# Attention's background work in another order, queries in a scaled tile of their own, and bias loads at fixed places

## The chip, the cores and the metric

The kernel runs on one core of one Trainium2 chip. Engines: TensorE (PE), VectorE (DVE), ScalarE (ACT), GpSimd (POOL) and SyncE (SP, which here only issues DMAs). The metric is device time in microseconds, the median of several runs.

## What is computed

A two-layer decoder trunk on 512 tokens of 1024 features, float32 in and out. Layer 0 is a short gated convolution and a squared-ReLU MLP. Its output is normalised once and projected into one set of keys and values for the attention of layer 1. That attention has 16 heads of 64 in 4 groups, and three branches that share the queries: compressed blocks, selected blocks and a window. A relative-position bias is added to every logit. A second MLP and a final norm follow. The part that matters here, cut to its core:

```python
def compress_blocks(t, pe, w1, w2):      # t: (S, G, 64) raw keys or raw values
    chunks = t.reshape(S // 16, 16, G, 64)
    blocks = concat([chunks[:-1], chunks[1:]]) + pe        # 31 blocks of 32 tokens
    return silu(flat(blocks) @ w1) @ w2                    # the "block MLP": 2048 -> 256 -> 64

kv = (h @ w_kv).reshape(S, 6, G, 64)     # raw k, raw v, selected k, v, window k, v
k_cmp, v_cmp = compress_blocks(kv[:, 0], ...), compress_blocks(kv[:, 1], ...)
q, gates = split(h @ w_qg); q = q * 64 ** -0.5
for branch in (compressed, selected, window):
    p = softmax(q @ k.T + bias)          # causal
    o += gate[branch] * (p @ v)
x = x + o @ w_o
```

With 8 blocks of 64 tokens and the 16 best to be taken, every block is selected, so the selected branch is full causal attention.

## The kernel before, in words

**Numbers.** Every large product is done in float16 halves: a float32 operand is split into a high part (ScalarE, a scaled copy) and a low part (VectorE, `x*scale - high`), and PE does three matmuls, high by high, high by low, low by high (`mm3`, L355 to L358).

**Weights.** A list of pieces of 512 KB is written out in the order of use (L105 to L132). SP loads them, three buffers ahead (`load_piece`). `convert_piece` splits one into `whi` (L202) and `wlo` (L203). `next_piece` hands out the next one; `ahead_fine` (L714) converts the piece behind it in halves, as a generator that the caller steps between matmuls.

**The lead-in of attention** (L926) runs in a row: keys of the two full branches, queries of group 0, values of both, gates.

**Items and background.** After that the work of a group is cut into items. A `Full` item is one block of 128 queries, one branch and as many heads as fit in 512 columns of logits; a `Cmp` item is one block of 128 queries and two groups against the 31 compressed blocks. There are 96 items: 22 of group 0, 22 of group 1, 26 of group 2 with four `Cmp` among them, 26 of group 3 with four. Each item goes through stages `st0` to `st4`, and the loop at L1164 interleaves them: in turn i it runs `st0` of item i, `st1` of item i − 2, `st2` of i − 3, `st3` of i − 4, `st4` of i − 6.

- `st0`: scores on PE into bank b (two buffers; L998, L999), then on VectorE the bias and the row minimum in one instruction per head (L1006: out `at_s`, in `b` and `T`), then the exponent on ScalarE (L1008: out `at_p`).
- `st1`: transposes on PE into bank c (L1014) and the high part on ScalarE (L1017). `st2`: the low part on VectorE (L1020).
- `st3`: the product with the values on PE into bank d (L1033 to L1035), scaling on VectorE (L951, `o_t`), sums on POOL (L953, L956). `st4`: transposes (L967) and the split into `big` for the output projection.

Between items a generator, `background()` (L1147), is stepped for as long as a credit lasts. A step of it is some matmuls with a price (0.65 for one chunk of a projection, 0.42 for one of the block MLP), and each turn adds to the credit (L1174). Its order: raw keys, queries 1, block MLP of the keys (`phi(0)`), raw values, queries 2, block MLP of the values (`phi(1)`), queries 3, then, when groups 0 and 1 are finished (`o1`), the first half of the output projection. An item that needs something not yet done runs the background until it is.

**Queries** (L775). The projection lands in banks a. Per pair of heads VectorE scales it into a tile of 512 columns from the rotating pool `at_s` (L688, three buffers, the same name as the logits'). Per head, ScalarE writes the high half into `Q` (L785), and POOL the low half (L786), both from that tile. **Raw keys and values** (L793) go through `at_s` too (L804), are split into `kr_hl` and moved by DMA into `big`, which the block MLP reads. **The block MLP** (L818) accumulates its two halves in two banks a. **Bias tiles** `T` hold four heads' biases for one group; `load_T` issues their load on ScalarE's queue ahead of item 11, 35 and 60.

The framework that records the kernel orders each engine's instructions itself; `tc.issue_after(x)` keeps an instruction behind another one.

## Time and profile before

| | us |
|---|---|
| runs shown: 1113.25, 1115.03, 1116.88, median | 1115.03 |
| profiled execution, its own time | 1114.4 |
| its span, first to last instruction | 1112.5 |
| PE busy | 1091.4 |
| VectorE busy | 869.6 |
| ScalarE busy | 572.4 |
| POOL busy | 58.6 |

Attention's items run from about 549 to 760 us of the span. Lines are those of the kernel before. In a row of a view, `out<-in` are the program's tiles, x is a count, and what stands behind `<-` in brackets ended the engine's idle time. A matmul's end is modelled and matmuls are pipelined, so short waits of PE do not show as idle time.

### The profile page before, as it was taken

To read this page: it belongs to the slowest core of one execution; us is meant where nothing else is said; L and a number is where in the kernel's file an instruction comes from. 1 tells how busy PE (TensorE), PEld (TensorE's weight loads), DVE (VectorE), ACT (ScalarE), POOL (GpSimd) and SP (SyncE) were. 2 spreads that over 40 slices of the span, in tenths; PEclk is the share of its full clock that TensorE was granted. 3 is DMA by queue.
4 is the path that set the end of the run, shared out by engine and by line. 5 is a ranking of instruction groups with operands and counts; after the bars stand their busy time and mean duration, and the time that the engine had idled before them with its cause. 6 is when DMAs were issued, how large, how long until landed. Compare 5 with 4: busy or idle time off the path is not lost.

```text
span 1112.5 us, 20040 instructions
## 1 busy us (share of the span) xinstructions
PE 1091.4 (98%) x7960; PEld 694.1 (62%) x7960; DVE 869.6 (78%) x1627; ACT 572.4 (51%) x923; POOL 58.6 (5%) x75
## 2 busy tenths in 40 slices
PE   9999999999999999999999999899999999999996
PEld 4444444446884448875767676675444788445895
DVE  5755457987998677969588889997998698865776
ACT  4622235545343444447578787875754433352353
POOL 1000000000000000000102021212000000000020
PEclk9999999999999999999999999999999999999998
DMA  6433335543334333313334241112653333330221
GB/s 215 131 98 99 110 96 151 154 125 105 111 118 119 103 98 106 103 30 111 118 98 135 68 128 59 39 40 71 182 158 101 101 120 112 108 94 1 96 77 76
DMA packets 149708, 115.74 MB, mean 104 GB/s; under 512 B 8700, under 2 KB 146640, under 8 KB 149616
## 3 DMA queue, kind: packets, MB, share of 16 engines
q1 hardware_dynamic: 146624, 108.88, 32.2%
q10 hardware_dynamic: 2608, 4.97, 1.4%
q8 instruction: 62, 1.02, 0.4%
q0 software_dynamic: 384, 0.63, 0.2%
q14 instruction: 30, 0.25, 0.1%
HBM read 110.22 MB, written 2.14 MB: 101 GB/s over the span
## 4 chain that ended last, share of the span: by engine, by line
PE 86%; DVE 7%; ACT 3%; issue 2%; POOL 1%; DMA 0%; DVEq 0%; ACTq 0%; SPq 0%
PE a L582 8%; PE c L582 8%; PE a L357 6%; PE a L356 6%; PE a L358 6%; PE b L582 6%; PE c L356 6%; PE c L358 6%; PE c L357 6%; PE b L358 6%; PE b L357 5%; PE b L356 5%; PE d L582 4%; PE e L582 2%; PE c L1014 2%
## 5 line engine op out<-in xcount | busy, mean ns | idle before, releaser
L202 ACT ACTIVATE whi<-wst 128x1024 f16<-128x1024 f32 (+3 forms) x172 | 144.3, 854 | 188.1 <-PE b L357 66.4
L203 DVE SCALAR_TENSOR_TENSOR wlo<-wst,whi 128x1024 f16<-128x1024 f32 (+3 forms) x172 | 169.5, 996 | 44.8 <-ACT whi L202 44.5
L582 PEld LDWEIGHTS <-whi 128*128 128x128 f16 x1792 | 175.3, 98 | 20.6
L358 PEld LDWEIGHTS <-wlo 128*128 128x128 f16 x1024 | 100.3, 98 | 111.5 <-issue 0.5
L357 PEld LDWEIGHTS <-whi 128*128 128x128 f16 x1024 | 100.2, 98 | 108.7 <-issue 2.8
L356 PEld LDWEIGHTS <-whi 128*128 128x128 f16 x1024 | 100.4, 98 | 107.9 <-issue 0.9
L189 ACT ACTIVATE whi<-wst 128x1792 f16<-128x1792 f32 x64 | 108.5, 1700 | 109.2 <-DVE wst L187 43.6
L190 DVE SCALAR_TENSOR_TENSOR wlo<-wst,whi 128x1792 f16<-128x1792 f32 x64 | 129.0, 2018 | 14.4 <-ACT whi L189 14.4
L187 DVE TENSOR_TENSOR wst<-wst 128x256 f32<-128x256 f32 x256 | 95.7, 421 | 19.5 <-DMA wst<-mlp_w_dram 18.2
L533 DVE TENSOR_TENSOR rl<-ml_z,rh 128x1792 f16<-128x1792 f32 x32 | 64.8, 2024 | 44.7 <-ACT rh L532 44.7
L582 PEld LDWEIGHTS <-wlo 128*128 128x128 f16 x896 | 87.7, 98 | 10.8 <-issue 0.2
L532 ACT ACTIVATE rh<-ml_z 128x1792 f16<-128x1792 f32 x32 | 54.3, 1696 | 57.2 <-DVE ml_z L531 57.2
L1008 ACT ACTIVATE at_p<-at_s,at_m 128x384 f32<-128x384 f32 (+3 forms) x128 | 70.8, 554 | 21.4 <-DVE at_m L1006 20.5
L357 PE MATMUL b<-xsl,whi 128*128 128x512 f16 x208 | 78.8, 379 | 0.0
L358 PE MATMUL b<-xsh,wlo 128*128 128x512 f16 x208 | 78.8, 379 | 0.0
L356 PE MATMUL b<-xsh,whi 128*128 128x512 f16 x208 | 78.7, 379 | 0.0
L356 PE MATMUL c<-xsh,whi 128*128 128x512 f16 x192 | 72.8, 379 | 0.0
L357 PE MATMUL c<-xsl,whi 128*128 128x512 f16 x192 | 72.8, 379 | 0.0
L358 PE MATMUL c<-xsh,wlo 128*128 128x512 f16 x192 | 72.8, 379 | 0.0
L582 PE MATMUL c<-rl,whi 128*128 128x256 f16 x256 | 69.8, 273 | 0.0
L582 PE MATMUL c<-rh,whi 128*128 128x256 f16 x256 | 69.8, 273 | 0.0
L582 PE MATMUL c<-rh,wlo 128*128 128x256 f16 x256 | 69.8, 273 | 0.0
(318 smaller groups left out, 2549.0 us busy)
## 6 DMA issues: line engine op xcount, KB each, us to landing
wst<-mlp_w_dram SPq DMA_DIRECT2D x256, 256.0 KB, 3.3
wst<-a_w_in_dram SPq DMA_DIRECT2D x18, 512.0 KB, 3.6
wst<-w_kv_dram SPq DMA_DIRECT2D x12, 512.0 KB, 3.6
T<-ext_d ACTq DMA_DIRECT2D x4, 1056.0 KB, 6.1
wst<-a_w_out_dram SPq DMA_DIRECT2D x8, 512.0 KB, 3.4
wst<-b_w_qg_dram SPq DMA_DIRECT2D x8, 512.0 KB, 3.6
wst<-b_w_o_dram SPq DMA_DIRECT2D x8, 512.0 KB, 3.3
wst<-a_w_in_dram SPq DMA_DIRECT2D x7, 384.0 KB, 5.0
```

The source lines that it names most:

```text
L187: DVE.tensor_tensor(b[:, :, o], b[:, :, x], b[:, :, y], op=e)
L189: ACT.activation(hi, b[:, :, 1:], AF.Copy, scale=sc)
L190: DVE.scalar_tensor_tensor(lo, b[:, :, 1:], sc, hi, op0=OP.mult, op1=OP.subtract)
L202: ACT.activation(hi[:, s:e], w, AF.Copy, scale=sc)
L203: DVE.scalar_tensor_tensor(lo[:, s:e], w, sc, hi[:, s:e], op0=OP.mult, op1=OP.subtract)
L356: PE.matmul(ps, w[0], xs[0], start=start, stop=False)
L357: PE.matmul(ps, w[0], xs[1], start=False, stop=False)
L358: return PE.matmul(ps, w[1], xs[0], start=False, stop=stop)
L532: ACT.activation(rh[0][:, p], z[:, 1:8], AF.Copy)
L533: DVE.tensor_tensor(rh[1][:, p], z[:, 1:8], rh[0][:, p], op=OP.subtract)
L582: mm = PE.matmul(acc7[i], wl if n == 1 else wh, xl if n == 2 else xh, stop=c == 7 and n == 2, start=c == 0 and n == 0 and not other, skip_ ...
L1008: ACT.activation(self.p[:, w], lg[:, w], AF.Exp, bias=mn[:, j:j + 1], scale=-1.0, accum_out=l[:, br * 4 + h:br * 4 + h + 1])
```

## The change

- Weight pieces of the keys' block MLP and of the raw values are listed alternately, and `in_turn(phi(0), raw(1))` steps the two generators alternately. Since two generators are then open, the running conversion is held in one place (`fine`) and drained before the next piece is handed out.
- The block MLP's two halves share one bank e in place of two banks a.
- Queries are scaled into `q_t`, a tile of two times 512 columns with one buffer; raw keys and values and the second block MLP use the same name. The four splits into high and low halves are queued (`later`), and the loop runs one per item. An item waits for the heads that it uses. The low half of groups 1 and 2 is on VectorE, of groups 0 and 3 on POOL.
- The bias loads are issued behind the exponent of items 8, 29 and 58.
- The first four `Cmp` items stand behind items 4, 7, 10 and 13 of group 2 in place of 9 to 12. The credit per item is 1.14, 0.9 and 0.68 in place of 1.03, 0.78, 0.8 and 0.65.

```diff
-    block(phi_k_w1, 0, SW, 0, 16)
+    for k in (0, 8):
+        block(phi_k_w1, 0, SW, k, 4)
+        cols(w_kv, 256, 256, SW, k // 2, 4)
+        block(phi_k_w1, 0, SW, k + 4, 4)
     cols(phi_k_w2, 0, 64, SW, 0, 2)
-    block(w_kv, 256)
...
         pos["use"] += 1
+        drain(fine[0])
         while i not in ready:
...
         def ahead_fine():
-            while pos["cv"] < min(pos["use"] + AHEAD, len(pieces)):
-                yield from convert_piece(512)
+            drain(fine[0])
+            def convert():
+                while pos["cv"] < min(pos["use"] + AHEAD, len(pieces)):
+                    yield from convert_piece(512)
+            fine[0] = convert()
+            return fine[0]
...
             q = ap.tile([128, 4, S], F16, name="Q", bufs=3)
+            t = ap.tile([128, 2, S], F32, name="q_t", bufs=1)
+            Qs[g] = q
+            def head(h):
+                m, s = h // 2, h % 2
+                r, o = slice(64 * s, 64 * s + 64), slice(64 - 64 * s, 128 - 64 * s)
+                ACT.activation(q[r, h], t[r, m], AF.Copy)
+                (POOL if g in (0, 3) else DVE).tensor_tensor(q[o, h], t[r, m], q[r, h], op=OP.subtract)
+                done.add(f"q{g}.{h}")
             for m in range(2):
-                t = scaled(po[m], rbq)
-                for s in range(2):
-                    h, r = 2 * m + s, slice(64 * s, 64 * s + 64)
-                    o = slice(64 - 64 * s, 128 - 64 * s)
-                    ACT.activation(q[r, h], t[r], AF.Copy)
-                    POOL.tensor_tensor(q[o, h], t[r], q[r, h], op=OP.subtract)
-                yield
-            Qs[g] = q
+                DVE.tensor_tensor(t[:, m], po[m], rbq, op=OP.mult)
+            for h in range(4):
+                if lead_in[0]:
+                    head(h)
+                else:
+                    later.append(lambda h=h: head(h))
+            yield
...
-            ph = [bank("a"), bank("a")]
+            pb = bank("e")
+            ph = [pb[:, 0:155], pb[:, 155:310]]
...
-        items += mixed(full(2, (2, 3, 0, 1)), {9 + qb: Cmp(0, qb) for qb in range(4)})
+        items += mixed(full(2, (2, 3, 0, 1)), {4 + 3 * qb: Cmp(0, qb) for qb in range(4)})
...
-        at_item = {11: lambda: load_T(1), 35: lambda: load_T(2), 60: lambda: load_T(3)}
+        at_item = {8: 1, 29: 2, 58: 3}
...
-            yield from marked("q1", queries(1))
-            yield from phi(0)
-            yield from raw(1)
-            yield from marked("q2", queries(2))
+            yield from queries(1)
+            yield from in_turn(phi(0), raw(1))
+            yield from queries(2)
...
-                at_item.get(i, lambda: None)()
                 items[i].st0()
+                if i in at_item:
+                    load_T(at_item[i], items[i].weighed)
...
+                if later:
+                    later.pop(0)()
-            credit += 1.03 if i < 44 else 0.78 if i < 53 else 0.8 if i < 66 else 0.65
+            credit += 1.14 if i < 44 else 0.9 if i < 50 else 0.68
```

More of the change, by code (lines that the diff above doesn't have):

```diff
@@ L144, in body @@
     staged, ready = {}, {}
+    fine = [iter(())]
     pos = {"dma": 0, "cv": 0, "use": 0}
@@ L216, in next_piece @@
         pos["use"] += 1
+        drain(fine[0])
         while i not in ready:
-            for _ in convert_piece():
-                pass
+            drain(convert_piece())
         return ready.pop(i)
@@ L353, in rstd, with mm3 @@
             self.r = rstd_of(p[:, 0:4])
-    def mm3(ps, w, xs, start, stop):
-        PE.matmul(ps, w[0], xs[0], start=start, stop=False)
-        PE.matmul(ps, w[0], xs[1], start=False, stop=False)
-        return PE.matmul(ps, w[1], xs[0], start=False, stop=stop)
+    def mm3(ps, w, xs, start, stop, **k):
+        PE.matmul(ps, w[0], xs[0], start=start, stop=False, **k)
+        PE.matmul(ps, w[0], xs[1], start=False, stop=False, **k)
+        return PE.matmul(ps, w[1], xs[0], start=False, stop=stop, **k)
     def pair(xs, ps, kn=8, mid=None):
@@ L648, in body @@
         VC = ap.tile([128, 2, G, 4, 64], F16, name="VC")
-        Qs = {}
+        Qs, later = {}, []
         TG, TC = {}, {}
@@ L658, in body, with load_T @@
         ot = None
-        def load_T(g):
+        def load_T(g, behind=None):
             t = ap.tile([128, 4, TW], F32, name="T", bufs=2)
-            nc.scalar.dma_start(t, bass.AP(tensor=ext_d.tensor, offset=ext_d.offset + 4 * g * EXT,
-                                           ap=[[1, 128], [EXT, 4], [1, TW]]))
+            with tc.issue_after(behind.ins) if behind else nullcontext():
+                nc.scalar.dma_start(t, bass.AP(tensor=ext_d.tensor, offset=ext_d.offset + 4 * g * EXT,
+                                               ap=[[1, 128], [EXT, 4], [1, TW]]))
             TG[g] = t
@@ L800, in raw @@
                 split_to(kr[:, 0, 4, at], kr[:, 1, 4, at], pet[:, which, 8 * half:8 * half + 8], SK)
+            t2 = ap.tile([128, 2, S], F32, name="q_t", bufs=1)
             for m in range(2):
-                t = ftile("at_s", 3)
+                t = t2[:, m]
                 by_stride = lambda a: a.rearrange("p (b r) -> p r b", r=16)
@@ L828, in phi @@
                     for m in range(2):
-                        o = ph[m][:, 0:155].rearrange("p (g j) -> p g j", g=5)
-                        mm3(o, [u[:, c, m * 128:(m + 1) * 128] for u in w], rhs, cc == 0, cc == 15)
+                        o = ph[m].rearrange("p (g j) -> p g j", g=5)
+                        mm3(o, [u[:, c, m * 128:(m + 1) * 128] for u in w], rhs, cc == 0 and m == 0, cc == 15,
+                            skip_group_check=m == 1)
                         next(cv, None)
@@ L874, in phi @@
                         PE.matmul(o, lh[1], w[0][:, m], start=False, stop=m == 1)
+                t4 = ap.tile([128, 2, S], F32, name="q_t", bufs=1).rearrange("p a (b h d) -> p (a b) h d", h=4, d=64)
                 for g in range(4):
-                    t = ftile("at_s", 3)[:, 0:256].rearrange("p (h d) -> p h d", h=4)
+                    t = t4[:, g]
                     DVE.tensor_tensor(t, pv[:, None, g * 64:(g + 1) * 64].to_broadcast([128, 4, 64]),
@@ L920, in out_proj, with in_turn @@
                 drain(cv)
+        def in_turn(*gens):
+            gens = list(gens)
+            while gens:
+                for k in list(gens):
+                    u = next(k, "end")
+                    if u == "end":
+                        gens.remove(k)
+                    else:
+                        yield u
         def marked(name, gen):
@@ L924, in marked @@
             done.add(name)
-        for k in (keys(0), keys(1), marked("q0", queries(0)), values(0), values(1), gates()):
+        for k in (keys(0), keys(1), queries(0), values(0), values(1), gates()):
             drain(k)
@@ L986, in need @@
             def need(self):
-                return [f"q{self.g}"]
+                return [f"q{self.g}.{self.heads[-1]}"]
             def st0(self):
@@ L1007, in st0 @@
                                                            -1.0 / SL, 3e38, OP.add, OP.min, mn[:, j:j + 1])
-                    ACT.activation(self.p[:, w], lg[:, w], AF.Exp, bias=mn[:, j:j + 1], scale=-1.0,
-                                   accum_out=l[:, br * 4 + h:br * 4 + h + 1])
+                    self.weighed = ACT.activation(self.p[:, w], lg[:, w], AF.Exp, bias=mn[:, j:j + 1], scale=-1.0,
+                                                  accum_out=l[:, br * 4 + h:br * 4 + h + 1])
             def st1(self):
@@ L1057, in need @@
             def need(self):
-                return [f"q{2 * self.gp}", f"q{2 * self.gp + 1}", "cmp"]
+                return [f"q{2 * self.gp}.3", f"q{2 * self.gp + 1}.3", "cmp"]
             def st0(self):
@@ L1148, in background @@
             yield from raw(0)
-            yield from marked("q1", queries(1))
-            yield from phi(0)
-            yield from raw(1)
-            yield from marked("q2", queries(2))
+            yield from queries(1)
+            yield from in_turn(phi(0), raw(1))
+            yield from queries(2)
             yield from marked("cmp", phi(1))
-            yield from marked("q3", queries(3))
+            yield from queries(3)
             while "o1" not in done:
@@ L1167, in body @@
                     while k not in done:
-                        if next(bg, "end") in ("wait", "end"):
+                        if later:
+                            later.pop(0)()
+                        elif next(bg, "end") in ("wait", "end"):
                             raise RuntimeError(k)
-                at_item.get(i, lambda: None)()
                 items[i].st0()
+                if i in at_item:
+                    load_T(at_item[i], items[i].weighed)
                 if i in copy_at:
                     copy_Tc(copy_at[i], items[i].biased)
-            credit += 1.03 if i < 44 else 0.78 if i < 53 else 0.8 if i < 66 else 0.65
+                if later:
+                    later.pop(0)()
+            credit += 1.14 if i < 44 else 0.9 if i < 50 else 0.68
             while credit > 0.0:
```

## The prediction

> **What bounds the kernel now.** I read the page first.

> ```profile
> span 1112.5 us, 20040 instructions
> PE 1091.4 (98%) x7960; PEld 694.1 (62%) x7960; DVE 869.6 (78%) x1627; ACT 572.4 (51%) x923; POOL 58.6 (5%) x75
> PE 86%; DVE 7%; ACT 3%; issue 2%; POOL 1%; DMA 0%; DVEq 0%; ACTq 0%; SPq 0%
> ```

> TensorE (PE) is busy 98% of the span and carries 86% of the chain of work that ended last. The change leaves every matmul in place, so it can only win or lose PE's idle time. Next, busy time by stage through the attention's item loop:

> ```profile
> 549.00:562.00 13.00, 13.00 (x86) 7.20 (x84) 7.69 (x22) 10.36 (x25) 0.00 (x0) 1.00 0.45 146
> 562.00:596.00 34.00, 32.73 (x379) 24.04 (x376) 28.36 (x82) 26.89 (x74) 6.44 (x6) 1.00 0.26 65
> 596.00:608.00 12.00, 9.60 (x128) 7.70 (x125) 11.76 (x36) 10.31 (x32) 0.73 (x1) 1.00 0.67 199
> 608.00:650.00 42.00, 41.68 (x430) 28.11 (x429) 36.04 (x109) 32.48 (x95) 2.19 (x3) 1.00 0.33 90
> 650.00:672.00 22.00, 20.64 (x281) 16.76 (x278) 18.91 (x50) 19.13 (x52) 6.35 (x7) 1.00 0.43 137
> 672.00:697.00 25.00, 24.34 (x291) 17.42 (x290) 24.59 (x79) 18.13 (x47) 5.31 (x7) 1.00 0.14 44
> 697.00:713.00 16.00, 12.81 (x149) 9.07 (x146) 14.54 (x48) 14.36 (x42) 7.32 (x7) 1.00 0.10 34
> 713.00:760.00 47.00, 46.46 (x546) 33.95 (x545) 45.82 (x146) 34.57 (x99) 7.75 (x13) 1.00 0.15 47
> sum 211.00, PE 201.24 PEld 144.25 DVE 187.71 ACT 166.21 POOL 36.09; mean PE 25.16 PEld 18.03 DVE 23.46 ACT 20.78 POOL 4.51
> ```

> Columns: stage, then busy PE, weight load, VectorE (DVE), ScalarE (ACT), GpSimd (POOL), the granted clock, DMA. PE is idle 211.00 − 201.24 = 9.8 us, most of it in four places: 1.3 in 562–596, 2.4 in 596–608, 1.4 in 650–672, 3.2 in 697–713. The clock is full throughout. This is a floor:

> ```profile
> 582.73 0.38 PE L356 MATMUL a<-xqh,whi 128*128 128x512 f16 x1
> 582.95 0.38 PE L357 MATMUL a<-xql,whi 128*128 128x512 f16 x1
> ```

> A matmul lasts 0.38 but the next starts 0.22 later, so each pause hides up to 0.16. Adding, over the 2265 matmuls of the stages above, the time from start to start beyond the median of their shape, I get 16.7 us. Between 9.8 and 16.7 lies all that can be won here, 0.9 to 1.5% of the span.

> What are the four pauses? First POOL's subtractions for the queries (timeline):

> ```profile
> 590.38 5.21 POOL L786 TENSOR_TENSOR Q<-at_s,Q 64x512 f16<-64x512 f32 x4 [8.82 <-ACT Q L785]
> 593.14 0.42 DVE L1006 CUSTOM_DVE_ANT_0 at_s<-b,T 128x256 f32<-128x256 f32 x1 [0.94 <-POOL Q L786]
> 595.61 0.43 DVE L1006 CUSTOM_DVE_ANT_0 at_s<-b,T 128x256 f32<-128x256 f32 x1 [0.65 <-POOL Q L786]
> 651.19 4.85 POOL L786 TENSOR_TENSOR Q<-at_s,Q 64x512 f16<-64x512 f32 x4
> 653.77 0.56 DVE L1006 CUSTOM_DVE_ANT_0 at_s<-b,T 128x384 f32<-128x384 f32 x1 [2.20 <-PE b L999]
> 656.07 0.56 DVE L1006 CUSTOM_DVE_ANT_0 at_s<-b,T 128x384 f32<-128x384 f32 x1 [0.48 <-POOL Q L786]
> 701.66 4.84 POOL L786 TENSOR_TENSOR Q<-at_s,Q 64x512 f16<-64x512 f32 x4 [3.42 <-issue]
> 704.07 0.42 DVE L1006 CUSTOM_DVE_ANT_0 at_s<-b,T 128x256 f32<-128x256 f32 x1 [1.24 <-POOL Q L786]
> ```

> `at_s` has three buffers, shared by the logits (L1006) and the scaled queries that POOL reads for 4.8 to 5.2 us. Two buffers are held that long, so VectorE waits for POOL (0.94, 0.65, 0.48, 1.24), and its 2.20 falls inside such a run too. PE's banks of scores then stay full. Second, 596–608: VectorE is busy 98%, PE 80%. The chain in that stretch says with what:

> ```profile
> by line: DVE wlo L203 32.6%; DVE at_s L1006 19.4%; DVE at_pl L1020 18.1%; issue 9.0%; DVE o_t L951 5.0%; ACT whi L202 4.4%; DVE big L796 4.0%; PE c L1014 2.5%; DVE at_m L1006 2.4%; DVE phi_w L855 1.0%; DVE rl L1040 1.0%; DVE rl L1041 0.7%;
> ```

> This is the keys' block MLP: each 512 KB piece of its weights costs VectorE two conversions but feeds only 24 matmuls of 155 columns. Third, 697–713: POOL again, and no background left for PE.

> **The change part by part.** Durations:

> ```profile
> L786 POOL TENSOR_TENSOR Q<-at_s,Q 64x512 f16<-64x512 f32 x12 | 14.2, 1185 | 13.0 <-ACT Q L785 8.8 <-issue 3.4
> L785 ACT ACTIVATE Q<-at_s 64x512 f16<-64x512 f32 x12 | 7.5, 625 | 0.3
> L730 DVE TENSOR_TENSOR KD<-at_s,KD 64x512 f16<-64x512 f32 x8 | 5.5, 684 | 0.1
> L203 DVE SCALAR_TENSOR_TENSOR wlo<-wst,whi 128x512 f16<-128x512 f32 x38 | 26.0, 696 | 3.3 <-ACT whi L202 3.0
> L1020 DVE SCALAR_TENSOR_TENSOR at_pl<-c,at_ph 128x512 f16<-128x512 f32 x54 | 36.9, 686 | 4.1 <-ACT at_ph L1017 4.0
> L1006 DVE CUSTOM_DVE_ANT_0 at_s<-b,T 128x512 f32<-128x512 f32 x32 | 21.7, 678 | 1.2 <-PE b L999 1.2
> L662 ACTq DMA_DIRECT2D T<-ext_d x4: 366/370/399, 496.8 to 647.9; - x4
> ```

> *Queries in a tile of their own (`q_t`).* The at_s waits on POOL (0.94 + 0.65 + 0.48 + 1.24 = 3.3 us of VectorE) have no cause left, nor has most of the 2.20. What is late next is the head itself, but the four heads now stand one per item, and an item needs its own heads only. Group 1: the later part of its pause spilled past 596, so I take −0.6 of 1.3. Group 2: −1.0 of 1.4. `q_t` has one buffer for queries, raw values and the second block MLP; in the built order each use stands at least ten VectorE instructions behind the last reader of the one before, so I cost that at 0 (ceiling: one head's 0.63 + 0.68).

> *Subtractions of groups 1 and 2 on VectorE.* Eight of the L730 form, 8 × 0.684 = 5.5 us. VectorE has 34.00 − 28.36 = 5.6 us free in 562–596 and 42.00 − 36.04 = 6.0 in 608–650, where they fall, so 0 on the path. Without that cover it is 5.5.

> *Block MLP in turn with raw values.* In the built orders I counted each engine's work between the 96 items' scores (count times start-to-start time, which is about 0.08 under the durations above for VectorE). Before, three items (24–26) have 1.7 us of PE against 5.1 of VectorE, the next three 10.2 against 6.4. After, no three of the first sixty have PE under 4.8, and VectorE is ahead of PE by at most 1.2. ScalarE is ahead by more than that once, by 3.4 in items 30–32 (the MLP's tanh, two splits of raw values). The 2.4 shrinks to what that leaves, 0.6 by the ratio of pause to excess before (2.4 of 3.4, and most of ScalarE's excess lies beside its free 34.00 − 26.89): −1.8. The weights come in the new order of use, so SP's queue waits no longer than now.

> *The gap before the output projection.* The credit is higher early (1.14) and lower late (0.68). Group 3's products are spent by item 61, and the projection cannot start before item 70. Eight items stand with no background: 11.3 us of PE, 16.3 of VectorE, 16.4 of ScalarE. Before, it is four. The two score banks let PE run two items ahead, 2 × 1.4 = 2.8, so 5.0 − 2.8 = 2.2 idle in place of 3.2: −1.0, with POOL's 4.84 now outside the path. This is the term I trust least.

> *Bias loads pinned.* Four T loads of 0.37 us issue remain. They land hundreds of matmuls before use in both orders: 0.

> *Bank e for the block MLP.* The same matmuls in another bank:

> ```profile
> PE a L356 <- DVE at_s L804: 0.8, 2, 0.5
> PE a L356 <- DVE at_s L688: 0.7, 2, 0.4
> ```

> The waits of projections for banks a are 0.8 and 0.7 in all; with the MLP in bank e one of the four has no cause left, and one can appear where group 2's products follow raw values. I take 0, 0.4 either way.

> Sum: −0.6 − 1.0 − 1.8 − 1.0 = −4.4 in idle as the windows show it. Hidden pauses shrink with them (16.7 to 9.8, a factor of 1.7), so −4.4 to −7.5; I take −5.0, near the lower since the gap is uncertain. Against the profiled execution's own time, 1114.4 (span 1112.5 and 1.9 around it), that is 1109.4. The runs' median is 1115.03, 0.6 above it, so I forecast **1110.0**.

> A measured price of sharing between POOL and VectorE, from the lead-in:

> ```profile
> 526.94 2.24 DVE L203 SCALAR_TENSOR_TENSOR wlo<-wst,whi 128x512 f16<-128x512 f32 x2
> 527.17 6.16 POOL L786 TENSOR_TENSOR Q<-at_s,Q 64x512 f16<-64x512 f32 x4 [521.99 <-ACT Q L785]
> 529.73 2.58 DVE L203 SCALAR_TENSOR_TENSOR wlo<-wst,whi 128x512 f16<-128x512 f32 x2 [0.55 <-ACT whi L202]
> ```

> Two conversions take 2.24 and 2.58 beside POOL's subtractions, against 2 × 0.70 elsewhere: 0.4 to 0.6 more for each. [...]

> ```profile
> L953 POOL TENSOR_TENSOR o<-o_t 128x256 f32<-128x256 f32 x13 | 9.5, 731 | 118.0 <-DVE o_t L951 100.6 <-DVE rl L1041 17.3
> ```

> **The rivals.**

> *The pauses only move* (0.25). The gap takes all its 5.0 (+1.8 on 3.2) and items 30–32 all their 3.4 (+1.0 on 2.4), while POOL's relief gives 2.6: 1114.4 + 0.2 + 0.6 = 1115.2. For it: summed over stretches of four items, the larger of PE's and VectorE's work is 198 us in both orders. Against: PE's pauses came with lumps, and these are smaller.

> *VectorE sets the pace* (0.13, slower). The 5.5 us of subtractions lie on the path and the relief is used up: 1114.4 + 5.5 + 0.6 = 1120.5. It decides where VectorE has no free time left. In 562–697 it is busy 28.36 + 11.76 + 36.04 + 18.91 + 24.59 = 119.7 of 135; with 5.5 more, and 4 less time, 96%. Against: in 713–760 it is at 97% and PE idles 0.5 of 47.

> *All lumps go* (0.14). Every stage runs like 713–760, 0.54 idle in 47, so 2.4 in 211 in place of 9.8, and hidden pauses with it: −7.4 to −11; about −9.5, 1105.5.

> *POOL's lock* (0.05). Group 3's four subtractions stay on POOL, one per item, and slow two VectorE instructions each by the 0.5 above, 4 × 2 × 0.5 = 4.0: 1114.0. Against: in the built order no weight conversion stands beside them. [...]

> **How the numbers follow.** The forecast has 0.43, 1107 to 1111.6. A measurement of this kernel can tell about 0.3% (3.3 us) from no change. Faster by more: 0.43 + 0.14 = 0.57. Within: 0.25 + 0.05 = 0.30. Slower by more: 0.13. The range leaves out the slower case and the far end of the best: 1103.5 to 1117.5. Its upper end is the first rival plus the half of the subtractions' unknown cost (2.4), its lower the third rival's −11.

> **What would show it.** Right: no wait of L1006 on POOL; the pause at 596–608 gone, with the VectorE share near 90% there; matmuls of 155 and of 512 columns alternating; PE idle over the item loop about 5. The gap shows as PE idle just ahead of the first output projection, 2 to 3 us. Wrong: VectorE over 97% for tens of us with PE waiting on at_s or at_pl; over 4 us idle in the gap; ScalarE's queue holding PE at the MLP's tail.

## The result and the profile after

Over seven runs each, the changed kernel takes 1120.19 us (median; 1116.42 to 1121.09), the kernel before 1115.05: a ratio of 1.004, 95% interval 1.003 to 1.0051. It is 5 us slower where I had forecast 5 us faster. The profiled execution took 1119.04 us. (One run came at 1116.42, the other six at 1119 to 1121. Its mean granted clock was 0.998, theirs 0.994 to 0.996, so it seems to have been spared the half clock that is described below; it left no trace to read.) Lines of the changed kernel are numbered some 30 higher: the bias is L1040, the logits' exponent L1042, the split L381 and L383, the load of T L667.

The page's totals and the chain by engine:

```profile
span 1117.2 us, 20022 instructions
PE 1092.1 (98%) x7960; PEld 694.0 (62%) x7960; DVE 873.6 (78%) x1635; ACT 572.1 (51%) x923; POOL 47.9 (4%) x67
PE 83%; DVE 8%; ACT 4%; issue 3%; DMA 1%; SPq 0%; ACTq 0%; DVEq 0%
```

As many matmuls as before, busy as long to within 0.7 us, in a span 4.7 us longer. POOL's work shrank as announced. "DMA 1%" is new in the chain: something now waits for a transfer. By stage (stage, PE, weight load, VectorE, ScalarE, POOL, granted clock, DMA):

```profile
549.00:562.00 13.00, 13.00 (x86) 7.32 (x85) 8.42 (x21) 9.93 (x23) 0.00 (x0) 1.00 0.40 122
562.00:596.00 34.00, 29.68 (x291) 19.93 (x290) 25.53 (x69) 22.65 (x61) 1.46 (x2) 0.95 0.39 97
596.00:608.00 12.00, 11.06 (x137) 8.63 (x135) 9.53 (x32) 8.83 (x26) 0.71 (x1) 1.00 0.16 46
608.00:650.00 42.00, 40.26 (x440) 28.25 (x439) 38.24 (x108) 32.40 (x94) 2.59 (x4) 1.00 0.46 129
650.00:672.00 22.00, 20.57 (x293) 17.37 (x291) 21.67 (x63) 20.35 (x60) 1.66 (x3) 1.00 0.38 121
672.00:697.00 25.00, 24.23 (x278) 16.62 (x277) 24.47 (x72) 18.36 (x45) 3.61 (x5) 1.00 0.27 87
697.00:713.00 16.00, 12.84 (x159) 9.64 (x158) 14.14 (x56) 14.84 (x50) 7.88 (x7) 1.00 0.01 3
713.00:760.00 47.00, 46.05 (x531) 32.99 (x530) 44.65 (x140) 34.05 (x94) 6.54 (x12) 1.00 0.13 39
```

The loss stands in one row. In 562–596 PE idles 34.00 − 29.68 = 4.3 us (before: 1.3), VectorE and ScalarE are busy *less* than before, and the clock is 0.95 where it was 1.00. The pause near 600 shrank from 2.4 to 0.9, and in VectorE's waits of 549 to 760 the bias has one row left, none on POOL:

```profile
DVE at_s L1040 <- PE b L1033: 4.0, 5, 1.1
```

What happened in 562–596, from the timeline (start, duration, engine, line):

```profile
567.09 1.81 SPq L832 DMA_DIRECT2D big<-kr_hl  x1
568.02 0.37 ACTq L667 DMA_DIRECT2D T<-ext_d  x1
568.95 0.61 SPq L833 DMA_DIRECT2D big<-kr_hl  x1
...
571.76 0.38 PE L360 MATMUL a<-xqh,whi 128*128 128x512 f16 x1
...
575.27 0.63 ACT L381 ACTIVATE kr_hl<-q_t 128x512 f16<-128x512 f32 x1 [6.18 <-DMA big<-kr_hl]
...
576.34 0.20 PE L1067 MATMUL d<-VT,at_ph 128*128 128x64 f16 x1 [4.20 <-ACT at_ph L1051]
```

Read it from the bottom. PE waits 4.20 us for `at_ph`, which ScalarE writes. ScalarE stands 6.18 us at the second half of the raw keys' split: the split has one `kr_hl` buffer, which SP's copies into `big` still read. It kept to its order: the transposes for the next `at_ph` were done at 569.50, but ScalarE began it at 575.81, behind the split. Those six copies were issued from 564.4 to 568.95; in their midst, at 568.02, ScalarE issued group 1's bias load, pinned there by the change. The DMA queues from 570 to 573:

```profile
DMA packets 375, 0.79 MB, mean 264 GB/s; under 512 B 0, under 2 KB 0, under 8 KB 375
q10 hardware_dynamic: 375, 0.79, 99.6%
```

Queue q10 is ScalarE's, with the load of T (1056 KB). SP's queue q1 has no row: it moved nothing in these 3 us. Finer windows of the same stretch show a second price:

```profile
570.00:575.00 5.00, 2.14 (x10) 0.78 (x8) 0.70 (x2) 0.00 (x0) 0.00 (x0) 1.00 1.05 272
575.00:577.50 2.50, 1.16 (x9) 0.66 (x10) 1.57 (x3) 2.23 (x9) 0.00 (x0) 1.00 0.30 95
577.50:581.00 3.50, 3.50 (x28) 2.63 (x27) 2.18 (x8) 2.75 (x9) 0.00 (x0) 0.52 0.61 137
581.00:583.00 2.00, 2.00 (x25) 1.33 (x23) 1.74 (x4) 1.75 (x5) 0.73 (x1) 1.00 0.13 22
```

After the pause the granted clock is 0.52 over 3.5 us: PE is "busy" throughout, but a 128x512 matmul follows another after 0.41 us (578.84 and 579.25) where it took 0.22 ahead of the pause: 1.7 us lost.

**Theory A**: the pinned load shuts out the raw keys' copies, ScalarE waits for its one `kr_hl` buffer, PE stands 4.2 us and then runs 3.4 us at half clock. **Theory B**: the 5.5 us of subtractions moved to VectorE lie on the path (my slower rival, priced at 1120.5, the size that came). **Theory C**: the late stages cost it, above all the gap ahead of the output projection.

### The profile page after: what moved, and what is told of

Same layout as the page of the kernel before. It is cut to its first block, busy times and chain, and to the rows that moved or that the text cites. A ratio compares the mean times of both kernels' runs of the same rounds, so it can differ in the third digit from the quotient of the medians.

```text
span 1117.2 us, 20022 instructions
## 1 busy us (share of the span) xinstructions
PE 1092.1 (98%) x7960; PEld 694.0 (62%) x7960; DVE 873.6 (78%) x1635; ACT 572.1 (51%) x923; POOL 47.9 (4%) x67
## 4 chain that ended last, share of the span: by engine, by line
PE 83%; DVE 8%; ACT 4%; issue 3%; DMA 1%; SPq 0%; ACTq 0%; DVEq 0%
PE a L586 8%; PE c L586 7%; PE b L586 6%; PE c L361 6%; PE c L362 6%; PE c L360 6%; PE a L361 5%; PE b L362 5%; PE b L361 5%; PE a L362 5%; PE b L360 5%; PE a L360 5%; PE d L586 4%; PE e L586 2%; DVE at_s L1040 2%
## 5 line engine op out<-in xcount | busy, mean ns | idle before, releaser
L1042 ACT ACTIVATE at_p<-at_s,at_m 128x384 f32<-128x384 f32 (+3 forms) x128 | 71.0, 556 | 23.7 <-DVE at_m L1040 22.0
```

The lines of the kernel that those rows point to most:

```text
L1042: self.weighed = ACT.activation(self.p[:, w], lg[:, w], AF.Exp, bias=mn[:, j:j + 1], scale=-1.0, accum_out=l[:, br * 4 + h:br * 4 + h + 1])
```

## The experiments

All times are medians, beside 1114.7 to 1115.4 us of the kernel before on the same chip; "vs before" is the ratio to it with its interval. The kernel before itself differs by 0.7 us from chip to chip, so differences of less than that between two rows are read from the ratios.

| kernel | us | vs before |
|---|---|---|
| T's pins removed | 1114.78 | 1.0001 [0.9992, 1.001] |
| T(1) pinned behind item 13 | 1115.19 | 1.0007 [0.9998, 1.0016] |
| own kr_hl halves | 1114.66 | 1.0002 [0.9993, 1.0011] |
| before + pin of T(1) | 1119.73 | 1.0052 [1.0039, 1.0066] |
| half of T(1) at item 8 | 1119.64 | 1.0037 [1.0023, 1.0051] |
| a quarter of T(1) at item 8 | 1116.19 | 1.0008 [0.9999, 1.0016] |
| own halves, late credit 0.45 | 1113.38 | 0.9991 [0.9982, 0.9999] |
| own halves, subtractions on POOL | 1114.96 | 1.0 [0.9991, 1.0009] |
| own halves, no turns | 1114.9 | 1.0002 [0.9993, 1.0011] |
| own halves, credit 1.1/0.9/0.45 | 1114.48 | 0.9998 [0.9989, 1.0007] |
| own halves, credit 1.1/0.9/0.55 | 1111.61 | 0.9968 [0.9956, 0.9981] |
| the same, T's pins removed | 1110.45 | 0.9958 [0.9945, 0.997] |

**1. The pins removed.**

```diff
-        at_item = {8: 1, 29: 2, 58: 3}
+        at_item = {11: 1, 35: 2, 60: 3}
...
+                if i in at_item:
+                    load_T(at_item[i])
                 items[i].st0()
-                if i in at_item:
-                    load_T(at_item[i], items[i].weighed)
```

> The changed kernel, with its bias loads (T) free of their pins again, called for at items 11, 35 and 60 as before; the scheduler then issues group 1's load in the lead-in, well ahead of the raw keys' copies. Theory A (the pinned load of 1056 KB at 568 us runs into the raw keys' copies on SP's queue, ScalarE waits in order for the one kr_hl buffer, PE stands for 4.4 us and its clock is then halved for 3.4 us): the pause at 571.8 to 577 and the 0.5 clock are gone, VectorE's subtractions stay, and the time falls by 5 to 6.5 us, to 1113.5 to 1115.2. Theory B (the 5.5 us of subtractions on VectorE are on the path): 1119 to 1121, as the changed kernel. Theory C (the late stages, the gap before the output projection, are what cost): 1119 to 1121.

It took 1114.78 us. T(1) is now issued at 508.2, in the lead-in, as before. Its window and its wait:

```profile
562.00:596.00 34.00, 32.99 (x355) 22.95 (x354) 29.82 (x82) 26.54 (x70) 1.46 (x2) 1.00 0.26 65
...
ACT kr_hl L381 <- DMA big<-kr_hl: 0.7, 1, 0.7
```

PE's idle time is 1.0, the clock whole, ScalarE's wait 0.7 instead of 6.2. The loss is gone with the subtractions still on VectorE and the late stages as they were: theories B and C fall.

**2. One number: the pin five items later.** `at_item = {13: 1, ...}`; the load then stands behind the second split in ScalarE's order.

> The changed kernel with one number changed: group 1's bias load is pinned behind item 13's exponent in place of item 8's, after the second kr_hl split in ScalarE's order. Theory A: the raw keys' copies have SP's queue to themselves, the pause at 572 goes, 1113.5 to 1115.5. If a pin as such costs, wherever it stands (the load in ScalarE's queue ahead of its own reader): 1118 or more. Theories B and C: 1119 to 1121.

It took 1115.19. A pin as such costs nothing to speak of; its place does.

**3. The load stays, the wait goes.** The tile has room for both halves:

```diff
-                hl = ap.tile([128, 4, S], F16, name="kr_hl", bufs=1)[:, 0:2]
+                hl = (hl2 := ap.tile([128, 4, S], F16, name="kr_hl", bufs=1) if m == 0 else hl2)[:, 2 * m:2 * m + 2]
```

> The changed kernel with the pinned load where it is, but the two halves of the raw values' split get a half of the kr_hl tile each (the tile has room for both), so ScalarE's second split waits for no copy. Theory A: the copies are still slow beside the load (7 to 8 us to land), but nobody in front of PE waits for them; the pause and the half clock go, 1113.5 to 1116. A rival of A, that the load itself (not ScalarE's wait) holds PE, for example by what ScalarE or VectorE read then: 1118 to 1120. Theories B and C: 1119 to 1121.

It took 1114.66, though the collision is still there. The DMA issues of 563 to 582 (KB each, median us to landing):

```profile
T<-ext_d ACTq DMA_DIRECT2D x1, 1056.0 KB, 8.4
big<-kr_hl SPq DMA_DIRECT2D x4, 128.0 KB, 5.1
...
big<-kr_hl SPq DMA_DIRECT2D x4, 120.0 KB, 4.8
big<-kr_hl SPq DMA_DIRECT2D x4, 7.8 KB, 6.5
```

The load, issued at 568.82, runs beside the copies still, and they take 5 us to land (2.4 in the run with the pins removed). Nothing in front of PE waits for them now, so it costs nothing: ScalarE's wait is the link, not the slow copies.

**4. The kernel before with the pin alone.**

```diff
-        at_item = {11: lambda: load_T(1), 35: lambda: load_T(2), 60: lambda: load_T(3)}
+        at_item = {35: lambda: load_T(2), 60: lambda: load_T(3)}
...
                 items[i].st0()
+                if i == 8:
+                    load_T(1, items[i].weighed)
```

> The kernel before, with one thing of the change: group 1's bias load pinned behind item 8's exponent; in ScalarE's order it then stands ahead of the second kr_hl split, as in the changed kernel. Subtractions stay on POOL, the block MLP stays after the raw values. Theory A: the collision comes here too, with a PE pause of 3 to 5 us near 570 and a half clock behind it if the pause is long enough: 1118 to 1122. Theories B and C: 1115, as before.

It took 1119.73, 0.52% over the kernel before: this one edit brings the whole loss of the change. The timeline has the same row with the old line numbers:

```profile
579.16 0.20 PE L1034 MATMUL d<-VT,at_ph 128*128 128x64 f16 x1 [4.13 <-ACT at_ph L1018]
```

**5 and 6. A part of the load at item 8, the rest at item 13** (`load_T` gets a first head and a count; one `kr_hl` buffer as in the changed kernel).

> The changed kernel, with group 1's bias load cut in two: heads 0 and 1 (528 KB) behind item 8's exponent as now, heads 2 and 3 behind item 13's. kr_hl is one buffer as in the changed kernel, so ScalarE's second split still waits for the copies. Theory A, with the pause as long as the bytes ahead of the copies: a pause of about half, 2 to 2.5 us, too short for a half clock, so 1116 to 1117.5. If any load there costs the whole pause, whatever its size: 1119 to 1121. If half a load finds room beside the copies: 1114.5 to 1115.5.

> As the run with half a load, with one head (264 KB) of group 1's bias behind item 8's exponent and three behind item 13's; kr_hl is one buffer. ScalarE waited 6.2 us for the copies beside 1056 KB, 4.3 beside 528, 0.7 beside none. Theory A refined (the copies wait for the load's bytes, PE's pause is what ScalarE's wait leaves of its reserve, and from about 4 us of pause on the clock is halved as well, which cost 3.4 us at half in the changed kernel and 6.8 with half a load): ScalarE waits 2 to 3 us, PE stands 1 to 2.5, the clock stays whole, and the time is 1115 to 1117. If a load there costs the same whatever its size: 1119 to 1121.

Half took 1119.64, by the ratios as slow as the whole load (1.0037 against 1.004, intervals overlapping): not what theory A gave (1116 to 1117.5; that a pause of 2 to 2.5 us would leave the clock whole was my estimate, and this run had 3.87). Its windows say why:

```profile
570.00:574.00 4.00, 1.48 (x7) 0.49 (x5) 0.00 (x0) 0.62 (x2) 0.00 (x0) 1.00 0.96 258
574.00:575.00 1.00, 0.00 (x0) 0.00 (x0) 0.95 (x2) 1.00 (x6) 0.00 (x0) 0.51 0.00 1
575.00:581.00 6.00, 5.65 (x28) 3.48 (x29) 3.61 (x10) 3.82 (x13) 0.00 (x0) 0.51 0.40 87
```

ScalarE's wait did fall, from 6.2 to 4.3, but PE's only from 4.20 to 3.87: it stood some 0.7 us earlier, at transposes that wait for VectorE, which had itself stood 4.6 us for the same split of ScalarE's. And the half clock came 3.5 us earlier and lasted from 574 to 581, twice as long. A quarter took 1116.19, as expected: ScalarE waits 3.1, PE 1.91, and the clock stays whole:

```profile
575.00:577.00 2.00, 0.09 (x2) 0.05 (x1) 1.57 (x6) 2.00 (x10) 0.00 (x0) 1.00 0.27 62
577.00:581.00 4.00, 3.41 (x38) 2.33 (x39) 3.53 (x7) 2.77 (x6) 0.28 (x1) 1.00 0.47 100
```

So ScalarE's wait grows with the bytes (0.7, 3.1, 4.3, 6.2 us for 0, 264, 528, 1056 KB), while the time also contains a step for the clock. Against the kernel before on its own chip, a quarter costs 0.8 us (an amount whose interval reaches down to nothing), half 4.4 and the whole 5.1. The parts (PE's pause, and half of the time at half clock) don't add exactly: 4.20 + 1.7 is 5.9 for the whole, and 3.87 + 2.9 is 6.8 for the half. That at half clock the other engines catch up and later pauses are spared is only argued.

**7. The gap before the output projection**: own halves, and the credit 0.45 instead of 0.68 for items 50 to 69.

> The changed kernel with a half of the kr_hl tile for each split (the run with own halves, 1114.66 us, in which PE idled 2.2 us at 697 to 713), and one thing more: the credit of items 50 to 69 is 0.45 in place of 0.68, so group 3's products last to about item 69 and the late items are not without background. If the gap ahead of the output projection is an amount of its own, as the prediction had it: 1.5 to 3 us less, 1111.7 to 1113.2. If pauses only move (the same matmuls are missing where they now stand, items 50 to 60): 1114 to 1115.2.

It took 1113.38, 1.3 less than with own halves alone, a little short of the expected 1.5 to 3. The pause at 697–713 did not shrink (16.00 − 13.20 = 2.8; with own halves alone 2.2), the one at 672–697 did (0.4; with own halves alone 1.75).

**8. The subtractions back on POOL**: own halves, and `POOL.tensor_tensor` for every group.

> The changed kernel with own halves, and the eight subtractions of groups 1 and 2 back on POOL (still in q_t, one head per item). If VectorE's 5.5 us of subtractions are on the path, in part or wholly: 1109 to 1113. If they are hidden, as the prediction costed them: 1114 to 1115.5. If POOL's heads are waited for again (scores that wait for POOL, as before): 1115.5 to 1117.

1114.96, no difference. In 562–596 VectorE is busy 28.59 instead of 30.22, and PE 33.28 instead of 33.17: hidden, as costed. On POOL, one head per item, they cost no time either, though in 650–672 PE idles 22.00 − 19.34 = 2.7 us instead of 1.7.

**9. No turns**: own halves, with `phi(0)` then `raw(1)`, and the weights in that order.

> The changed kernel with own halves, and the block MLP not in turn with the raw values: first phi(0), then raw(1), with the weights streamed in that order. If taking turns saved what the prediction gave it (1.8 us of the pause near 600): 1116 to 1117. If the pause only moved: 1114 to 1115.2. In the built order the three items short of matmuls near item 24 do not come back in this kernel, so a third outcome is 1112 to 1114.

1114.9, the same within 0.3. Its windows where the pause was:

```profile
596.00:608.00 12.00, 9.68 (x110) 7.21 (x111) 11.66 (x35) 10.90 (x35) 0.74 (x1) 1.00 0.44 134
608.00:650.00 42.00, 41.60 (x456) 29.46 (x454) 35.62 (x101) 31.95 (x88) 2.19 (x3) 1.00 0.34 92
```

The pause at 596–608 comes back to 12.00 − 9.68 = 2.3 us, from 1.4 with the turns. Behind it, in 608–650, PE idles 42.00 − 41.60 = 0.4 us, where with the turns it idles 1.35. So the turns move about 1 us of that pause, they don't remove it.

**10 and 11. An evener credit.** `1.1 if i < 44 else 0.9 if i < 50 else 0.45 if i < 70 else 0.68`, then 0.55 for 0.45.

> The changed kernel with own halves and an evener credit throughout: 1.1 to item 43, 0.9 to 49, 0.45 to 69, 0.68 after. Summed over stretches of four items, the largest of the three engines' work is 199 us in the built order in place of 205. If that sum is what decides: 1109 to 1112. If the pauses are shorter than four items and only move: 1113.5 to 1115.

> The run with the even credit (1114.48 us) with one number changed, 0.55 in place of 0.45 for items 50 to 69. There group 3's four heads came only at item 70, PE waited 0.87 and 1.5 us for POOL's subtractions, idled 4.3 us in 697 to 713 and had its clock at 0.89 there; in the built order here they stand at item 67. If that pause and the clock behind it were what took the gain of the even credit back: 1111 to 1113. If pauses only move: 1114 to 1115.

The first took 1114.48, as if pauses only moved. Its PE idled 4.1 us from 549 to 697 (7.0 with own halves alone) and then 4.3 in 697–713. Its windows, and its PE waits in 697–713:

```profile
706.00:708.00 2.00, 0.85 (x14) 0.60 (x14) 1.44 (x3) 1.46 (x3) 1.84 (x3) 1.00 0.00 0
708.00:710.00 2.00, 1.25 (x7) 1.06 (x8) 0.62 (x3) 0.23 (x2) 1.85 (x3) 0.75 0.00 0
710.00:713.00 3.00, 3.00 (x24) 1.86 (x23) 2.46 (x6) 1.90 (x5) 1.56 (x1) 0.59 0.37 128
```

```profile
PE b L1032 <- POOL Q L798: 2.4, 2, 1.5
```

Group 3's heads came only when item 70 needed them; PE waited for POOL, and the clock was at half for some 3.5 us. With 0.55 they come three items earlier, and it took 1111.61: 2.9 us for one number. The clock is not the whole of it: two of the eleven runs with 0.45 had a mean clock of 0.998 and still took 1113.6.

**12. All together.**

> All that the runs so far speak for: the changed kernel with own kr_hl halves, bias loads free of their pins, and the credit 1.1, 0.9, 0.55, 0.68. If the gains add: 1110.5 to 1112.5, under both kernels. If pauses only move: 1114 to 1115.

1110.45 us, faster than both kernels. Freeing the pins gives 1.2 over run 11, though no split waits for a copy there; which of the three pins pays was not tried. Its sum of 549 to 760:

```profile
sum 211.00, PE 203.34 PEld 146.56 DVE 194.53 ACT 166.28 POOL 26.77; mean PE 25.42 PEld 18.32 DVE 24.32 ACT 20.79 POOL 3.35
```

PE idles 7.7 us, against 9.8 before.

## Why the prediction was wrong

**The step that failed** is "Bias loads pinned … They land hundreds of matmuls before use in both orders: 0". The load does land in time, and T's reader never waits. I costed the load by its own reader and its 0.37 us of issue, not by what it shares the DMA engines with: the change moved 1056 KB from the lead-in (508) to 568, into the middle of the copies that free `kr_hl`, with ScalarE, which kept to its order, standing 6.18 us behind them. Undoing the pin, moving it, or freeing ScalarE each bring the time back to within 0.6 us of the kernel before on the same chip; the pin alone on the kernel before costs 5.07 (1119.73 − 1114.66). My own list of what would prove it wrong came near ("ScalarE's queue holding PE"), at the wrong place.

**The other terms** can be read from the run with own halves, where that event is gone. Its stages from 562 on:

```profile
562.00:596.00 34.00, 33.17 (x361) 23.21 (x359) 30.22 (x84) 27.32 (x73) 1.45 (x2) 1.00 0.40 97
596.00:608.00 12.00, 10.64 (x134) 8.35 (x132) 9.48 (x30) 8.70 (x25) 0.73 (x1) 1.00 0.28 77
608.00:650.00 42.00, 40.65 (x461) 29.49 (x459) 38.03 (x106) 33.46 (x99) 2.19 (x3) 1.00 0.42 120
650.00:672.00 22.00, 20.29 (x288) 15.77 (x285) 21.62 (x67) 19.61 (x57) 1.87 (x4) 1.00 0.39 122
672.00:697.00 25.00, 23.25 (x276) 16.67 (x273) 24.05 (x72) 18.98 (x45) 7.25 (x8) 1.00 0.27 87
697.00:713.00 16.00, 13.80 (x150) 9.83 (x148) 14.68 (x52) 13.49 (x46) 4.80 (x5) 1.00 0.00 1
713.00:760.00 47.00, 45.91 (x540) 32.99 (x538) 44.16 (x142) 34.75 (x98) 7.39 (x12) 1.00 0.16 47
```

| stage | PE idle before | with own halves | difference | predicted |
|---|---|---|---|---|
| 562–596 (group 1's heads) | 1.27 | 0.83 | −0.4 | −0.6 |
| 596–608 (turns) | 2.40 | 1.36 | −1.0 | −1.8 |
| 608–650 | 0.32 | 1.35 | +1.0 | 0 |
| 650–672 (group 2's heads) | 1.36 | 1.71 | +0.4 | −1.0 |
| 672–697 | 0.66 | 1.75 | +1.1 | 0 |
| 697–713 (gap) | 3.19 | 2.20 | −1.0 | −1.0 |
| 713–760 | 0.54 | 1.09 | +0.6 | 0 |

*Heads, turns and gap.* Three of the four predicted gains arrived in their windows, wholly or in part, 2.5 us together, and 3.0 came back in the other four. The sum is +0.5 in idle and nothing in time: without the load's collision, this is the first rival, "the pauses only move" (1115.2; measured 1114.66). Run 9 shows it for the turns: pause back, the new one in 608–650 gone, time unchanged. I had named a remnant there, items 30–32 with ScalarE ahead by 3.4, and let it count inside the 2.4 instead of as a new pause. The new pause does come with the turns; that it is that remnant is not shown, and the waits of PE that the trace lists there are for VectorE (`at_pl` 0.8 us, `q_t` 0.5). For the gap I compared two windows and not two stages: the background ends at item 61, so the gap begins before 697. That it is worth something was right (run 7, −1.3; runs 10 and 11 more), only the change doesn't do it.

*POOL's waits.* Right that no L1040 waits on POOL any more. That this is worth 1.6 us did not show: with own halves those waits are gone too, and the time is that of the kernel before. Run 8 doesn't bring them back, since the queries stay in `q_t`; it shows that with that tile and one head per item the choice of engine is free. Which of the two makes POOL harmless was not tried.

*POOL's lock.* No run shows what makes weight conversions longer beside POOL's subtractions (1.30 us in place of 0.70 at 705.58 in the run with credit 0.45). In the changed kernel group 3's four subtractions ran from 698.62 to 703.46 with no conversion beside them, and VectorE's instructions took there what they take elsewhere (`at_pl` of 512 columns 0.69 us, against 0.686 on average): the rival's 4.0 us were not spent.

*Subtractions on VectorE: 0.* Right (run 8). My slower rival had the right total, 1120.5, by the wrong mechanism; VectorE is busy 25.53 of 34 where the time was lost. A total that fits shows no cause.

*`q_t` with one buffer, bank e.* Not tried apart; together with all else but the load they leave the time where it was.

*The floor.* "Between 9.8 and 16.7 lies all that can be won" was not contradicted (the best kernel wins 4.8), but I never asked what could be lost. The range's upper end came from pauses of the trace of before, where the clock was full throughout; a new pause of 4 us and the clock behind it were in no row.

*Slips in the sums.* The first rival gives POOL's relief 2.6 where my own terms give 0.6 + 1.0; half of the subtractions' 5.5 is 2.75 and not 2.4; and the third rival's 7.4 times the factor of 1.7 is 12.6, not 11. The range's upper end would be 1118 with the second, so none of them explains the miss.

## What to carry to other kernels

When a large load moves, look at what else is in flight at its new time and who waits for *that*, even if its own reader has ample time. Here a tile with a single buffer turned a slow transfer (7.9 us) into a stop of ScalarE (6.18 us) and of PE behind it (4.20 us). Removing a pause counts only when the sum over all stages falls; compare stages, not windows, and test each part alone.

## What the runs showed of the hardware

*One large load held up another queue.* In 570 to 573 the load of T had 99.6% of the DMA engines' time and SP's queue moved nothing. Of the six copies that free `kr_hl`, the first four landed after 2.4 to 3.7 us; the last two, issued at 567.09 and 568.95, took 7.9 and 6.2. Whether the copies' packets waited behind the load's is not shown: SP's issue at 567.09 took 1.81 us where its neighbours took 0.6, so the copies may have been late already in being handed to the engines. Which it is was not tried. The 120 KB copies' landing times (shortest, median, longest), in the changed kernel and then with T's pins removed:

```profile
DMA to landing us min/median/max: 2.4/2.4/7.9
```

```profile
DMA to landing us min/median/max: 2.4/2.4/2.7
```
